# The two ends of a SwiGLU block in an encoder layer: weight sums of the down product formed during gate/up, the first columns of gate/up made earlier, operands of down asked for ahead, the residual added on VectorE

## The chip, the core and the metric

One core of a Trainium2 chip runs the whole layer in one launch. The metric is the device time of that core in microseconds (us). The kernel before takes 3411.99 us in the median of three runs (3408.57 to 3416.47).

## What is computed

One encoder layer over 2304 tokens (a prompt of 2048 and a sample of 256), in float32. With `h = rms_norm(x)`, a combined projection feeds latent attention (8 heads, dense softmax) and a bidirectional SSD scan; their results are mixed by one output projection, and then comes the part that the change is about:

```python
x = x + concat([mla_out, ssd_out]) @ w_out
h = rms_norm(x, ffn_norm_g)
x = x + (silu(h @ w_gate) * (h @ w_up)) @ w_down      # D = 1024, D_FF = 2816
y = rms_norm(x, final_norm_g)
```

## The kernel before

The tokens are 18 tiles of 128. Every float32 product is made from operands that are split in two (a rounded high part, and the rest as a low part), with three matmuls for one (`mm3`, L113 to L115): ScalarE copies the high part, and VectorE subtracts it from the source for the low one (L937 and L938, L1126 and L1127, L1134 and L1135). The stages follow each other; the program is written as one list of operations, each engine gets its own order from a scheduler, and memory that a pool of an earlier stage held is a wait for the later one.

- Projection and scan. Its last tiles store `d_sb` and `d_y` (L564, L569).
- Attention. `load_head` (L654 to L657) loads a head's keys `k` (from `d_k` and `d_kr`) and values; `score` (L113 to L115) makes logits in the two banks `ma` and `mb`, and a reduction takes their maximum `mx` (L679). The pools of this stage lie on the left side of the memory, `mpool` (L613), which holds the attention's output, on the right.
- Output projection, tile by tile: `gather` (L805 to L832) finishes a tile of the scan with two matmuls into bank `o` (L819), `turned` (L840) transposes it through the banks `ta` and `tb`, `project` (L846 to L853) multiplies it by `w_out`, adds the residual and stores the tile in `d_x2`. The first four tiles are also normalised there and stay in memory.
- Gate/up. The tokens are three parts `s` of two halves of three tiles. A Winograd form of Strassen's scheme makes seven products (`MS`), each for the gate and the up weights (`u`), for 11 column blocks `j`: 462 groups of 12 matmuls of 128x384. `turned` (L932, L933) makes the columns `hB0` and `hB1` of a part by 24 transposes for each half through the banks `tb` and `o`, `tokens` (L952 to L963) forms sums of them and splits them into `U`, `weights` (L973 to L992) loads `rawf`, forms sums of it and splits them into `ws`, `group` multiplies (L1005), and `out` (L1026) stores the seven operands of the down product in `d_A`. `weights` runs seven groups ahead.
- Down. Again seven products `m`, in the order 1, 6, 5, 7, 3, 4, 2. Of each, `columns` makes 11 weight blocks `wd`: for 1, 2 and 3 a block as it is loaded (L1105), for 5, 7, 6 and 4 a sum of two, two, three and four blocks, formed on GpSimd (L1114 to L1124). Then nine operands `as` are loaded and split (`operand`, L1132 to L1135), each is multiplied by the 11 blocks (33 matmuls of 128x512), and VectorE adds the result into `acc` (L1147). In `m` = 3 the residual is added, on GpSimd (L1176).

Of the kernel before, what the change touches and what calls it, by code (L numbers as in the profile page):

```python
# [20 lines left out]
P = 128  # L21
D = 1024
# [18 lines left out]
def hymba_kernel(ctx: ExitStack, tc: tile.TileContext, io, seqs, dbg=None):  # L41
# [570 lines left out]
    op = pool(ctx, "e_o", 4, side="right")  # L612
    mpool = pool(mixer, "mla", 1, side="right")  # L613
    mla = {}
# [159 lines left out]


    with ExitStack() as ph:
        st = pool(ph, "d_st", 2)
# [66 lines left out]
        def project(c, mT):  # L844
            xt = mp.tile([P, D], F32, name="xr", tag="xr")
# [16 lines left out]
        first_xs = {}  # L862
        order = [c for c, _ in falling(1)]
        ys, mTs = {}, {}
# [21 lines left out]
    HK = KD // 2  # L886
    G = 3
    W = G * P
    assert NT % (2 * G) == 0
    parts = [(order[i:i + G], order[i + G:i + 2 * G]) for i in range(0, NT, 2 * G)]  # L890
    MS = (1, 2, 6, 5, 3, 7, 4)
    d_A = {(m, s): dram.tile([P, HF, G, P], F32, name=f"d_A{m}_{s}") for m in MS for s in range(len(parts))}


    with ExitStack() as ph:
        hb = pool(ph, "e_hb", 1)
        up = pool(ph, "e_u", 1)
        rp = pool(ph, "e_raw", 3)
        wp = pool(ph, "e_w", 8)
# [22 lines left out]

        H = {}

        def turned(s, half):

            xs = normed(parts[s][half])
            h = hb.tile([P, KD, W], F32, name=f"hB{half}", tag=f"hB{half}")
            for k in range(KD):
                ps = bank(("tb", "o")[k % 2])  # L930
                for i in range(G):
                    nc.tensor.transpose(ps[:, i * P:(i + 1) * P], xs[i][:, k * P:(k + 1) * P], ident)  # L932
                nc.scalar.activation(h[:, k, :], ps[:, :W], AF.Copy, scale=g_ffn[:, k:k + 1])  # L933
            H[s, half] = h

# [134 lines left out]
        for a in groups[:AHEAD]:  # L1070
            weights(*a)
        turned(0, 0)
        tokens(0, 1)
# [17 lines left out]
    with ExitStack() as ph:  # L1091
        rp = pool(ph, "f_raw", 6)
        ap = pool(ph, "f_a", 2)
# [8 lines left out]

        def block(j, i, half):
            raw = rp.tile([P, 512], F32, name="rawd", tag="rawd")
            nc.sync.dma_start(raw, io["w_down"][j + i * HF, :, half * 512:(half + 1) * 512])  # L1105
            return raw

        def columns(m, j):

            if m in (1, 2, 3):  # L1110
                src = block(j, *{1: (0, 0), 2: (1, 0), 3: (1, 1)}[m])
            elif m == 7:
                src, b = block(j, 0, 1), block(j, 1, 1)
                nc.gpsimd.tensor_tensor(src, b, src, op=ALU.subtract)  # L1114
            else:
                b = block(j, 0, 0)
                src = block(j, 0, 1)
                nc.gpsimd.tensor_tensor(src, src, b, op=ALU.subtract)  # L1118
                if m != 5:
                    b = block(j, 1, 1)  # L1120
                    nc.gpsimd.tensor_tensor(src, b, src, op=ALU.subtract)
                if m == 4:
                    b = block(j, 1, 0)
                    nc.gpsimd.tensor_tensor(src, b, src, op=ALU.subtract)  # L1124
            w = wp.tile([P, 2, 512], F32R, name="wd", tag="wd")
            nc.scalar.activation(w[:, 0], src, AF.Copy)  # L1126
            nc.vector.tensor_tensor(w[:, 1], src, f(w)[:, 0], op=ALU.subtract)  # L1127
            return w

        def operand(m, s, t):  # L1130
# [18 lines left out]
        L, R = slice(0, 512), slice(512, 1024)  # L1149
        for m in (1, 6, 5, 7, 3, 4, 2):  # L1150
            cols = [columns(m, j) for j in range(HF)]
            for s, (lo, hi) in enumerate(parts):
                for t in range(G):
                    a = operand(m, s, t)
                    ps = bank("m")
                    for j in range(HF):
                        mm3(ps, a[:, 0, j, :], a[:, 1, j, :], cols[j][:, 0], cols[j][:, 1], j == 0, j == HF - 1)
                    if m == 1:
                        for c in (lo[t], hi[t]):
                            acc[c] = cp.tile([P, D], F32, name=f"acc{c}", tag=f"acc{c}")  # L1160
                    y0, y1 = acc[lo[t]], acc[hi[t]]
                    if m == 1:
                        nc.scalar.activation(y0[:, L], ps, AF.Copy)
                    elif m == 6:
                        add(y1[:, L], ps, y0[:, L])
                    elif m == 5:
                        add(y0[:, R], ps, y1[:, L])
                    elif m == 7:
                        add(y1[:, R], ps, y0[:, R])
                        add(y1[:, L], ps, y1[:, L])  # L1170
                    elif m == 3:
                        add(y0[:, R], ps, y0[:, R])
                        for c in (hi[t], lo[t]):
                            xt = op.tile([P, D], F32, name="o", tag="o")
                            nc.sync.dma_start(xt, d_x2[c])
                            nc.gpsimd.tensor_tensor(acc[c], acc[c], xt, op=ALU.add)  # L1176
                    elif m == 4:
                        add(y1[:, L], ps, y1[:, L])
                        finish(hi[t], y1)
                    else:  # L1180
                        add(y0[:, L], ps, y0[:, L])
                        finish(lo[t], y0)

# [63 lines left out]
```

## Time and profile before

| | |
|---|---|
| median of the runs | 3411.99 us (3408.57, 3411.99, 3416.47) |
| the profiled execution | 3416.36 us, of which the span is 3414.7 us |
| busy over the span | TensorE 95%, VectorE 72%, ScalarE 50%, GpSimd 18% |
| projection and scan | 0 to 745 us |
| attention | 745 to 1619 us |
| output projection | 1619 to 1875 us |
| gate/up | 1875 to 2891 us |
| down | 2891 to 3415 us |

The profiled execution lies 4.4 us above the median, so a time worked out on its trace is 4.4 us too long for the runs. A busy TensorE is shown at the pace of its issue, and the stretches in which it is not busy are the ones to look at: the two at the ends of gate/up, and those in the down product.

### The profile page before, as it was taken

How to read it: one execution, taken by the hardware profiler on the slowest of the kernel's cores; microseconds unless marked ns; L12 is line 12 of the kernel's file. 1: busy time of each engine (PE TensorE's matmuls, PEld its weight loads, DVE VectorE, ACT ScalarE, POOL GpSimd, SP SyncE). 2: the span in 40 equal slices, each digit the busy share in tenths (PEclk: the TensorE clock that was granted, in tenths of full speed). 3: DMA queues.
4: the chain of work that ended last, by engine and by line, in shares of the span. 5: the costliest groups of instructions: out<-in, count | busy, mean ns of one | idle time of the engine just before them, and what ended most of it. 6: DMA issues, size and time to landing. Idle time of an engine off the chain costs nothing.

```text
span 3414.7 us, 48534 instructions
## 1 busy us (share of the span) xinstructions
PE 3244.2 (95%) x17817; PEld 2882.8 (84%) x17817; DVE 2456.1 (72%) x4396; ACT 1698.0 (50%) x3518; POOL 609.4 (18%) x597
## 2 busy tenths in 40 slices
PE   8998999879999999999799799999999999999988
PEld 7897988858888888887688699999999998778777
DVE  6445799978888888887854777787778776354566
ACT  5453444437777777777311545455544444222233
POOL 2222577750000000000310000000000000432630
PEclk9999999979999999999899899999999999999999
DMA  6565222231022111200642333333333333755664
GB/s 253 191 227 186 90 81 75 69 83 37 27 54 52 39 40 41 54 17 15 224 139 99 142 115 122 142 118 118 137 141 132 113 119 118 230 185 172 224 212 137
DMA packets 259166, 407.24 MB, mean 119 GB/s; under 512 B 21424, under 2 KB 170608, under 8 KB 256368
## 3 DMA queue, kind: packets, MB, share of 16 engines
q1 hardware_dynamic: 258928, 404.15, 35.5%
q8 instruction: 140, 2.29, 0.3%
q14 instruction: 98, 0.80, 0.1%
HBM read 274.98 MB, written 129.11 MB: 118 GB/s over the span
## 4 chain that ended last, share of the span: by engine, by line
PE 78%; DVE 11%; DMA 3%; POOL 3%; issue 3%; ACT 2%; SPq 0%; POOLq 0%; ACTq 0%; DVEq 0%
PE bank_mb L1005 8%; PE bank_ma L1005 8%; PE bank_ta L1005 8%; PE bank_ma L113 6%; PE bank_ma L115 6%; PE bank_ma L114 6%; PE bank_mb L113 5%; PE bank_mb L115 5%; PE bank_mb L114 5%; DVE Y L469 4%; PE bank_ta L721 4%; PE bank_o L729 3%; PE bank_o L730 3%; DMA rawd<-w_down 2%; PE bank_tb L721 2%
## 5 line engine op out<-in xcount | busy, mean ns | idle before, releaser
L938 DVE TENSOR_TENSOR ws<-rawf,ws 128x512 fp32r<-128x512 f32 x396 | 267.8, 687 | 97.2 <-ACT ws L937 95.3
L937 ACT ACTIVATE ws<-rawf 128x512 fp32r<-128x512 f32 x396 | 241.8, 627 | 171.7 <-PE bank_ta L1005 37.2
L1005 PE MATMUL bank_ma<-U,ws 128*128 128x384 f32 x1584 | 302.8, 338 | 6.4 <-ACT U L937 3.2
L1005 PE MATMUL bank_mb<-U,ws 128*128 128x384 f32 x1584 | 304.2, 336 | 2.8 <-ACT c L1014 2.5
L1005 PE MATMUL bank_ta<-U,ws 128*128 128x384 f32 x1584 | 297.3, 334 | 3.5 <-ACT U L937 3.0
L1005 PEld LDWEIGHTS bank_ma<-U,ws 128*128 128x128 f32 x1584 | 279.0, 190 | 8.0 <-ACT U L937 3.5
L129 DVE TENSOR_TENSOR pT<-bank_ta,pT 128x512 fp32r<-128x512 f32 (+1 forms) x352 | 239.6, 681 | 63.2 <-ACT pT L128 54.6
L1005 PEld LDWEIGHTS bank_mb<-U,ws 128*128 128x128 f32 x1584 | 277.4, 189 | 5.1 <-ACT c L1014 4.1
L1005 PEld LDWEIGHTS bank_ta<-U,ws 128*128 128x128 f32 x1584 | 276.7, 188 | 4.5 <-ACT U L937 3.3
L128 ACT ACTIVATE pT<-bank_ta 128x512 fp32r<-128x512 f32 (+1 forms) x352 | 209.1, 595 | 116.7 <-PE bank_ta L721 116.2
L1118 POOL TENSOR_TENSOR rawd<-rawd 128x512 f32<-128x512 f32 x33 | 51.5, 1559 | 1189.0 <-DMA rawd<-w_down 1188.6
L729 PE MATMUL bank_o<-pT,v 128*128 128x512 f32 x528 | 248.7, 471 | 1.9 <-ACT ot L736 1.9
L469 DVE SCALAR_TENSOR_TENSOR Y<-X,cw,Y 128x256 f32<-128x256 f32 x288 | 218.5, 815 | 22.9 <-POOL X L456 15.4
L679 DVE TENSOR_REDUCE mx<-bank_ma 128x1 f32<-128x512 f32 (+1 forms) x261 | 177.0, 678 | 50.1 <-PE bank_ma L115 49.5
L721 PE MATMUL bank_ta<-ident,pr 128*128 128x128 f32 x1388 | 210.6, 273 | 2.0 <-DVE pT L129 2.0
L721 PEld LDWEIGHTS bank_ta<-ident,pr 128*128 128x128 f32 x1388 | 170.5, 140 | 48.7 <-DVE pT L129 8.0
L730 PE MATMUL bank_o<-pT,v 128*128 128x512 f32 x528 | 206.2, 391 | 0.0
L1134 ACT ACTIVATE as<-rawa 128x1408 fp32r<-128x1408 f32 x63 | 86.7, 1378 | 225.6 <-PE bank_ma L115 108.6
L688 ACT ACTIVATE pr<-bank_mb,mx 128x512 f32<-128x512 f32 (+1 forms) x261 | 181.4, 695 | 7.9 <-DVE mx L679 4.8
L688 ACT ACTIVATE pr<-bank_ma,mx 128x512 f32<-128x512 f32 (+1 forms) x261 | 179.1, 686 | 6.4 <-DVE mx L707 5.5
L679 DVE TENSOR_REDUCE mx<-bank_mb 128x1 f32<-128x512 f32 (+1 forms) x261 | 176.9, 678 | 7.0 <-PE bank_mb L115 3.7
L752 POOL TENSOR_TENSOR mla<-lo,ri 128x256 f32<-128x256 f32 (+1 forms) x40 | 22.8, 570 | 855.6 <-DVE lo L751 842.5
(399 smaller groups left out, 8584.9 us busy)
## 6 DMA issues: line engine op xcount, KB each, us to landing
rawf<-w_gu SPq DMA_DIRECT2D x66, 1024.0 KB, 5.8
rawa<-d_A SPq DMA_DIRECT2D x63, 704.0 KB, 5.2
rawd<-w_down SPq DMA_DIRECT2D x154, 256.0 KB, 4.9
d_A<-c SPq DMA_DIRECT2D x132, 192.0 KB, 1.9
d_A<-s SPq DMA_DIRECT2D x99, 192.0 KB, 1.9
o<-d_x SPq DMA_DIRECT2D x32, 512.0 KB, 4.8
d_hT<-hT SPq DMA_DIRECT2D x7, 2048.0 KB, 12.9
hT<-d_hT SPq DMA_DIRECT2D x7, 2048.0 KB, 7.9
```

The costliest lines, as they stand in the source:

```text
L113: nc.tensor.matmul(ps, wh, xh, start=start, stop=False)
L114: nc.tensor.matmul(ps, wh, xl, start=False, stop=False)
L115: nc.tensor.matmul(ps, wl, xh, start=False, stop=stop)
L469: nc.vector.scalar_tensor_tensor(y[:, j, :], x[:, j, t:t + n], cw[:, j, t:t + 1], y[:, j, :], op0=ALU.mult, op1=ALU.add)
L679: nc.vector.tensor_reduce(mx[:, j:j + 1], ps[:, :m * P], axis=AX.X, op=ALU.max, negate=nch == 1)
L688: nc.scalar.activation(e[:, :m * P], ps[:, :m * P], AF.Exp, bias=bias, accum_out=rs[:, i, j:j + 1])
L721: nc.tensor.transpose(ps[:, i * P:(i + 1) * P], pr[i, kt // 4][:, kt % 4 * P:(kt % 4 + 1) * P], ident)
L729: nc.tensor.matmul(po[0][:, :n], v[:, s0 + kt, :], pT[:, 0, :n], start=kt == 0, stop=False)
L730: nc.tensor.matmul(po[0][:, :n], v[:, s0 + kt, :], pT[:, 1, :n], start=False, stop=kt == sn - 1)
L937: nc.scalar.activation(dst[:, 0], src, AF.Copy)
L938: nc.vector.tensor_tensor(dst[:, 1], src, f(dst)[:, 0], op=ALU.subtract)
L1005: nc.tensor.matmul(ps[:, :W], w[:, a, k, :], x[:, b, k, :], start=k + n == 0 and not more, stop=k == HK - 1 and n == 2, skip_group_check=more)
```

## The change

It has five parts. (1) The first half's columns are made in the output projection, by `columns_of`, right after the third tile; six tiles are normalised there instead of four, and `mpool` moves to the left side to make room for `hB0`. (2) `sums(j)` loads two rows of blocks of `w_down` during gate/up, forms four sums on GpSimd and stores them in `d_B`; down loads them from there. (3) In down the next operand is asked for one ahead, and the first five weight blocks of the next product two operands ahead of its start. (4) The operands `as` take the room of `hB0` and `hB1`, and the raw blocks get four buffers instead of six. (5) The residual is added on VectorE.

```diff
-    mpool = pool(mixer, "mla", 1, side="right")
+    mpool = pool(mixer, "mla", 1)
...
+    hbs = [pool(ctx, "e_hb0", 1, side="right")]
+    def columns_of(s, half, xs):
+        h = hbs[half].tile([P, KD, W], F32, name=f"hB{half}", tag="hB")
+        for k in range(KD):
+            ps = bank(("tb", "o")[k % 2])
+            for i in range(G):
+                nc.tensor.transpose(ps[:, i * P:(i + 1) * P], xs[i][:, k * P:(k + 1) * P], ident)
+            nc.scalar.activation(h[:, k, :], ps[:, :W], AF.Copy, scale=g_ffn[:, k:k + 1])
+        H[s, half] = h
...
-            if c in order[:4]:
+            if c in order[:2 * G]:
...
+            if c == order[G - 1]:
+                columns_of(0, 0, [first_xs.pop(t) for t in order[:G]])
...
+    hbs.append(pool(ctx, "e_hb1", 1, side="right"))
+    d_B = {m: dram.tile([P, HF, 512], F32, name=f"d_B{m}") for m in (4, 5, 6, 7)}
...
-        hb = pool(ph, "e_hb", 1)
+        rp = pool(ph, "e_raw", 3)
         up = pool(ph, "e_u", 1)
-        rp = pool(ph, "e_raw", 3)
...
+        def sums(j):
+            top, low = (op.tile([P, D], F32, name="o", tag="o") for _ in range(2))
+            nc.sync.dma_start(top, io["w_down"][j])
+            nc.sync.dma_start(low, io["w_down"][j + HF])
+            b11, b12, b21, b22 = top[:, :512], top[:, 512:], low[:, :512], low[:, 512:]
+            for m, out, x, y in ((5, b11, b12, b11), (7, b12, b22, b12), (6, b22, b22, b11), (4, b21, b21, b22)):
+                nc.gpsimd.tensor_tensor(out, x, y, op=ALU.subtract)
+                nc.sync.dma_start(d_B[m][:, j], out)
...
-        turned(0, 0)
...
+            if s + 1 == len(parts) and u and m == 1:
+                sums(j)
...
-        rp = pool(ph, "f_raw", 6)
+        rp = pool(ph, "f_raw", 4)
...
+        def columns(m, j):
             raw = rp.tile([P, 512], F32, name="rawd", tag="rawd")
+            if m in B:
+                i, half = B[m]
+                nc.sync.dma_start(raw, io["w_down"][j + i * HF, :, half * 512:(half + 1) * 512])
             else:
+                nc.sync.dma_start(raw, d_B[m][:, j])
...
-            a = ap.tile([P, 2, HF, P], F32R, name="as", tag="as")
+            a = hbs[n_a[0] % 2].tile([P, 2, HF, P], F32R, name="as", tag="hB")
...
+        prepare(1, AHEAD)
+        ahead = operand(*work[0])
+        for i, (m, s, t) in enumerate(work):
+            prepare(m, HF)
+            a = ahead
+            if i + 1 < len(work):
+                ahead = operand(*work[i + 1])
+            if i % n_m == n_m - 2 and i + 2 < len(work):
+                prepare(work[i + 2][0], AHEAD)
...
-                            nc.gpsimd.tensor_tensor(acc[c], acc[c], xt, op=ALU.add)
+                    nc.vector.tensor_tensor(acc[c], acc[c], xt, op=ALU.add)
```

How the engines' orders move shows at three places. The first is SyncE's queue at the end of the scan, one piece of the difference (`d_sb` and `d_y` are the scan's last stores, `k` and `v` the first head's loads, `q` its queries):

```order
+L564 DMA d_sb_169<-ns_7241 128x512
+L569 DMA d_y_134<-yo 128x512
+L564 DMA d_sb_170<-ns_7291 128x512
 L654 DMA k<-d_k_93 64x4608
 L655 DMA k<-d_kr 32x4608
 L657 DMA v<-d_v 128x18x128
-L569 DMA d_y_130<-yo 128x512
-L564 DMA d_sb_166<-ns_6999 128x512
-L473 DMA d_C_151<-Y 256x1x128
-L473 DMA d_C_152<-Y 256x1x128
```

The loads of the first head now stand behind the last store of the scan, where those of the second head stood; before they stood ahead of its last twelve stores (the rows with a minus are the first four of those).

The second is SyncE's queue in the last but one column blocks of part `s` = 1 of gate/up, of the change (L945 and L946 are the loads of `sums`, L950 its stores, L989 the weights' load, L1042 the stores of `d_A`):

```order
L989 DMA rawf<-w_gu 128x2x1024
L950 DMA d_B_19459<-o 128x512
L946 DMA o<-w_down 128x1024
L950 DMA d_B_19457<-o 128x512
L950 DMA d_B_19458<-o 128x512
L945 DMA o<-w_down 128x1024
L1042 DMA d_A_1_19455<-c_25329 128x384
L946 DMA o<-w_down 128x1024
L950 DMA d_B_19460<-o 128x512
L950 DMA d_B_19459<-o 128x512
```

None of the L945, L946 and L950 rows was there before. Although `sums` is written in part 2, all but the first of the 44 stores stand between the weights of `j` = 7 of part 1 and the end of that part.

The third is SyncE's queue at the start of down (the blocks of `m` = 1 are L1105 before and L1127 in the change, the operands L1132 and L1139, the last stores of gate/up L1026 and L1042). Before:

```order
L1132 DMA rawa<-d_A_0_19353 128x11x128 x2
L1026 DMA d_A_2_19358<-c_28846 128x384
L1105 DMA rawd<-w_down 128x512 x2
L1026 DMA d_A_2_19367<-s_28969 128x384
L1105 DMA rawd<-w_down 128x512 x4
L1132 DMA rawa<-d_A_0_19353 128x11x128
```

And in the change:

```order
L1127 DMA rawd<-w_down 128x512 x4
L1139 DMA rawa<-d_A_0_19436 128x11x128 x3
L1139 DMA rawa<-d_A_1_19437 128x11x128
L1042 DMA d_A_2_19456<-c_29009 128x384
L1042 DMA d_A_2_19447<-s_29096 128x384
L1042 DMA d_A_2_19444<-s_29097 128x384
L1042 DMA d_A_2_19453<-c_29023 128x384
L1127 DMA rawd<-w_down 128x512
L1042 DMA d_A_2_19441<-c_28975 128x384
L1127 DMA rawd<-w_down 128x512 x2
L1042 DMA d_A_2_19450<-s_29098 128x384
L1127 DMA rawd<-w_down 128x512 x2
```

Four operands now stand ahead of the last stores of gate/up, where two stood ahead of the last two of them; the fifth block and the later ones stand among and behind those stores, as the seventh and the later ones did (six had been loaded at the start of part 2).

## Rows read from the trace of the kernel before

**Rows 1.** The page's busy times, shares of the span and instructions of each engine.
```profile
PE 3244.2 (95%) x17817; PEld 2882.8 (84%) x17817; DVE 2456.1 (72%) x4396; ACT 1698.0 (50%) x3518; POOL 609.4 (18%) x597
```
**Rows 2.** The view by stretches of the whole span: stretch, its length, busy time (and count) of TensorE, its weight loads, VectorE, ScalarE and GpSimd, the granted clock, the DMA engines' busy share, GB/s.
```profile
745.00:765.00 20.00, 15.22 (x45) 10.69 (x45) 12.56 (x24) 10.74 (x30) 0.00 (x0) 0.67 0.80 195
765.00:1619.00 854.00, 845.80 (x4801) 692.17 (x4800) 702.98 (x1271) 659.68 (x1633) 21.80 (x38) 1.00 0.14 37
1619.00:1682.00 63.00, 43.97 (x173) 33.24 (x172) 55.05 (x97) 18.68 (x40) 28.81 (x22) 0.81 0.70 236
...
1875.00:1922.00 47.00, 24.49 (x105) 17.97 (x104) 36.23 (x62) 30.38 (x47) 0.00 (x0) 0.75 0.39 148
1922.00:2891.00 969.00, 966.01 (x5585) 962.78 (x5583) 731.46 (x1340) 460.95 (x872) 0.00 (x0) 1.00 0.34 123
2891.00:2906.00 15.00, 7.33 (x18) 5.12 (x17) 11.46 (x16) 8.40 (x12) 0.00 (x0) 0.66 1.06 322
...
2965.00:3000.00 35.00, 28.64 (x112) 22.23 (x111) 18.09 (x17) 11.95 (x16) 13.47 (x10) 0.90 0.75 237
...
3215.00:3295.00 80.00, 65.51 (x259) 50.95 (x258) 45.47 (x54) 20.15 (x25) 62.14 (x32) 0.91 0.80 255
```
**Rows 3.** The timeline of SyncE's queue at the end of the scan (start, length): the first head's keys, and the second head's behind the last store.
```profile
671.53 0.52 SPq L654 DMA_DIRECT2D k<-d_k  x1
...
747.30 0.32 SPq L564 DMA_DIRECT2D d_sb<-ns  x1
747.72 0.51 SPq L654 DMA_DIRECT2D k<-d_k  x1
748.29 0.57 SPq L655 DMA_DIRECT2D k<-d_kr  x1
```
**Rows 4.** The DMA issues from 665 to 700 us (the first head's rotary keys) and from 745 to 765 us (the second's): count, KB, us from issue to landing.
```profile
k<-d_kr SPq DMA_DIRECT2D x1, 576.0 KB, 11.8
...
k<-d_kr SPq DMA_DIRECT2D x1, 576.0 KB, 10.2
```
**Rows 5.** VectorE's timeline where the scan ends: attention's first maximum.
```profile
745.12 0.68 DVE L679 TENSOR_REDUCE mx<-bank_ma 128x1 f32<-128x512 f32 x1
```
**Rows 6.** The chain that ended last, where gate/up starts (start, length, what).
```profile
1874.71 0.24 PE bank_mb L115
...
1876.11 5.29 DMA rawf<-w_gu
...
1918.66 1.68 DVE U L938
1920.38 3.89 PE bank_ma L1005 x11
...
1939.15 4.16 PE bank_ta L1005 x24
```
**Rows 7.** The view by stretches again, of the blocks `j` = 8, 9 and 10 of part 1 and 0 and 1 of part 2 of gate/up.
```profile
2482.30:2511.50 29.20, 29.20 (x168) 29.20 (x169) 20.03 (x35) 12.31 (x24) 0.00 (x0) 1.00 0.46 167
2511.50:2540.60 29.10, 29.10 (x169) 29.10 (x169) 21.27 (x38) 13.49 (x26) 0.00 (x0) 1.00 0.32 119
2540.60:2569.80 29.20, 29.20 (x171) 29.20 (x170) 25.66 (x38) 18.73 (x28) 0.00 (x0) 1.00 0.33 122
2569.80:2599.90 30.10, 29.61 (x169) 28.97 (x168) 28.25 (x39) 14.47 (x26) 0.00 (x0) 1.00 0.44 151
2599.90:2629.10 29.20, 29.20 (x171) 29.20 (x170) 23.98 (x44) 13.73 (x26) 0.00 (x0) 1.00 0.37 137
```
**Rows 8.** Groups of instructions from 3184 to 3277 us, where GpSimd works 89 of 93 us: count, busy time, mean ns of one, idle time before and what ended it.
```profile
L1127 DVE TENSOR_TENSOR wd<-rawd,wd 128x512 fp32r<-128x512 f32 x10 | 19.0, 1912 | 33.0 <-ACT wd L1126 33.0
L1135 DVE TENSOR_TENSOR as<-rawa,as 128x1408 fp32r<-128x1408 f32 x10 | 25.0, 2498 | 1.8 <-ACT as L1134 1.6
L1147 DVE TENSOR_TENSOR acc<-bank_ma,acc 128x512 f32<-128x512 f32 x5 | 3.4, 683 | 5.4 <-PE bank_ma L115 5.4
```
**Rows 9.** The same kind of rows without GpSimd (gate/up's part 2, 2630 to 2860 us, and the operands' splits from 3300 to 3400 us), GpSimd's sums of two blocks over the whole span, and, of 2891 to 3415 us, two groups of 128x1024 (the final scaling, and the residual).
```profile
L938 DVE TENSOR_TENSOR ws<-rawf,ws 128x512 fp32r<-128x512 f32 x96 | 64.7, 688 | 31.5 <-ACT ws L937 31.2
...
L1135 DVE TENSOR_TENSOR as<-rawa,as 128x1408 fp32r<-128x1408 f32 x13 | 21.1, 1626 | 8.7 <-ACT as L1134 8.7
...
L1118 POOL TENSOR_TENSOR rawd<-rawd 128x512 f32<-128x512 f32 x33 | 51.5, 1559 | 1189.0 <-DMA rawd<-w_down 1188.6
...
L1143 DVE SCALAR_TENSOR_TENSOR acc<-acc,rs_y,gf 128x1024 f32<-128x1024 f32 x18 | 23.0, 1285 | 0.5
L1176 POOL TENSOR_TENSOR acc<-acc,o 128x1024 f32<-128x1024 f32 x18 | 52.1, 2904 | 17.5 <-DVE acc L1147 13.4 <-DMA o<-d_x 4.1
```
**Rows 10.** TensorE's timeline where down starts, and two of its last matmuls.
```profile
2886.64 4.67 PE L1005 MATMUL bank_ta<-U,ws 128*128 128x384 f32 x26
2897.88 0.79 PE L113 MATMUL bank_ma<-wd,as 128*128 128x512 f32 x1 [6.57 <-ACT as L1134]
...
3402.80 0.39 PE L114 MATMUL bank_ma<-wd,as 128*128 128x512 f32 x1
...
3405.07 0.39 PE L115 MATMUL bank_ma<-wd,as 128*128 128x512 f32 x1
```
**Rows 11.** The page's DMA issues of the two kinds of load in down: count, KB, us from issue to landing.
```profile
rawa<-d_A SPq DMA_DIRECT2D x63, 704.0 KB, 5.2
rawd<-w_down SPq DMA_DIRECT2D x154, 256.0 KB, 4.9
```

More of the change, by code (lines that the diff above doesn't have):

```diff
@@ L773, in hymba_kernel @@
                 step()
+    G = 3
+    W = G * P
+    assert NT % (2 * G) == 0
+    order = [c for c, _ in falling(1)]
+    parts = [(order[i:i + G], order[i + G:i + 2 * G]) for i in range(0, NT, 2 * G)]
+    hbs = [pool(ctx, "e_hb0", 1, side="right")]
+    H, first_xs = {}, {}
+    def columns_of(s, half, xs):
[6 more added lines that the diff above has]
+        H[s, half] = h
     with ExitStack() as ph:
@@ L844, in project @@
         def project(c, mT):
-            xt = mp.tile([P, D], F32, name="xr", tag="xr")
+            xt = st.tile([P, D], F32, name="xr", tag="rawo")
             nc.sync.dma_start(xt, tile_src[c])
@@ L860, in project @@
                 first_xs[c] = xn
-        first_xs = {}
-        order = [c for c, _ in falling(1)]
+            if c == order[G - 1]:
+                columns_of(0, 0, [first_xs.pop(t) for t in order[:G]])
         ys, mTs = {}, {}
@@ L886, in hymba_kernel @@
     HK = KD // 2
[L887 to L890, printed above, removed]
+    hbs.append(pool(ctx, "e_hb1", 1, side="right"))
     MS = (1, 2, 6, 5, 3, 7, 4)
     d_A = {(m, s): dram.tile([P, HF, G, P], F32, name=f"d_A{m}_{s}") for m in MS for s in range(len(parts))}
+    d_B = {m: dram.tile([P, HF, 512], F32, name=f"d_B{m}") for m in (4, 5, 6, 7)}
     with ExitStack() as ph:
-        hb = pool(ph, "e_hb", 1)
+        rp = pool(ph, "e_raw", 3)
         up = pool(ph, "e_u", 1)
-        rp = pool(ph, "e_raw", 3)
         wp = pool(ph, "e_w", 8)
@@ L921, in normed @@
             return xs
-        H = {}
         def turned(s, half):
[L927 to L934, printed above, removed]
+            columns_of(s, half, normed(parts[s][half]))
+        def sums(j):
[6 more added lines that the diff above has]
+                nc.sync.dma_start(d_B[m][:, j], out)
         def split(dst, src):
@@ L1101, in hymba_kernel @@
         acc = {}
-        def block(j, i, half):
+        B = {1: (0, 0), 2: (1, 0), 3: (1, 1)}
+        def columns(m, j):
             raw = rp.tile([P, 512], F32, name="rawd", tag="rawd")
[L1105 to L1114, printed above, removed]
-            else:
[L1116 to L1124, printed above, removed]
+            if m in B:
+                i, half = B[m]
+                nc.sync.dma_start(raw, io["w_down"][j + i * HF, :, half * 512:(half + 1) * 512])
+            else:
+                nc.sync.dma_start(raw, d_B[m][:, j])
             w = wp.tile([P, 2, 512], F32R, name="wd", tag="wd")
-            nc.scalar.activation(w[:, 0], src, AF.Copy)
-            nc.vector.tensor_tensor(w[:, 1], src, f(w)[:, 0], op=ALU.subtract)
+            nc.scalar.activation(w[:, 0], raw, AF.Copy)
+            nc.vector.tensor_tensor(w[:, 1], raw, f(w)[:, 0], op=ALU.subtract)
             return w
+        n_a = [0]
         def operand(m, s, t):
@@ L1132, in operand @@
             nc.sync.dma_start(raw, d_A[m, s][:, :, t])
-            a = ap.tile([P, 2, HF, P], F32R, name="as", tag="as")
+            n_a[0] += 1
+            a = hbs[n_a[0] % 2].tile([P, 2, HF, P], F32R, name="as", tag="hB")
             nc.scalar.activation(a[:, 0], raw, AF.Copy)
@@ L1149, in hymba_kernel @@
         L, R = slice(0, 512), slice(512, 1024)
[L1150 to L1175, printed above, removed]
-                            nc.gpsimd.tensor_tensor(acc[c], acc[c], xt, op=ALU.add)
[L1177 to L1182, printed above, removed]
@@ new lines, in hymba_kernel, with prepare @@
+        AHEAD = 5
+        work = [(m, s, t) for m in (1, 6, 5, 7, 3, 4, 2) for s in range(len(parts)) for t in range(G)]
+        n_m = len(parts) * G
+        cols = {m: [] for m, _, _ in work}
+        def prepare(m, upto):
+            while len(cols[m]) < upto:
+                cols[m].append(columns(m, len(cols[m])))
+        prepare(1, AHEAD)
+        ahead = operand(*work[0])
+        for i, (m, s, t) in enumerate(work):
+            lo, hi = parts[s]
+            prepare(m, HF)
[4 more added lines that the diff above has]
+                prepare(work[i + 2][0], AHEAD)
+            ps = bank("m")
+            for j in range(HF):
+                mm3(ps, a[:, 0, j, :], a[:, 1, j, :], cols[m][j][:, 0], cols[m][j][:, 1], j == 0, j == HF - 1)
+            if m == 1:
+                for c in (lo[t], hi[t]):
+                    acc[c] = cp.tile([P, D], F32, name=f"acc{c}", tag=f"acc{c}")
+            y0, y1 = acc[lo[t]], acc[hi[t]]
+            if m == 1:
+                nc.scalar.activation(y0[:, L], ps, AF.Copy)
+            elif m == 6:
+                add(y1[:, L], ps, y0[:, L])
+            elif m == 5:
+                add(y0[:, R], ps, y1[:, L])
+            elif m == 7:
+                add(y1[:, R], ps, y0[:, R])
+                add(y1[:, L], ps, y1[:, L])
+            elif m == 3:
+                add(y0[:, R], ps, y0[:, R])
+                for c in (hi[t], lo[t]):
+                    xt = op.tile([P, D], F32, name="o", tag="o")
+                    nc.sync.dma_start(xt, d_x2[c])
+                    nc.vector.tensor_tensor(acc[c], acc[c], xt, op=ALU.add)
+            elif m == 4:
+                add(y1[:, L], ps, y1[:, L])
+                finish(hi[t], y1)
+            else:
+                add(y0[:, L], ps, y0[:, L])
+                finish(lo[t], y0)
```

## The prediction

> **What bounds the kernel now.** I read the page's busy times first: TensorE is busy 95% of the span [rows 1], so the change can win only where TensorE stands still. The view by stretches says where that is [rows 2]. Attention (845.8 of 854 us) and gate/up from 1922 us on (966 of 969) are full. Idle time and a granted clock under 1.00 stand together at four places that the change touches: 745 to 765 us (15.2 of 20 busy, clock 0.67), 1619 to 1682 (44.0 of 63, 0.81), 1875 to 1922 (24.5 of 47, 0.75), and the down product, at its start (7.3 of 15, 0.66) and at two changes of product (28.6 of 35; 65.5 of 80). Then I read the timelines at these places, the chain that ended last, and the stretches of gate/up in which the sums will run, for what VectorE has left there.
>
> **Down: −36.** Two of its last matmuls, 3402.80 and 3405.07 us, lie ten steps apart [rows 10], so 0.227 us each, and 7 x 9 x 11 x 3 = 2079 of them need 472.5 us. The stage takes from 2891.3 (the end of the last group of gate/up, 2886.64 + 4.67) to about 3405.4: 514.1. So 41.6 us are lost: 6.6 before the first matmul (which waits for an operand's split), some 12 at the lower clock after it, about 10 at 2965 to 3000, about 21 at 3215 to 3295, where GpSimd's sums of three and four blocks and the residual run (62.1 of 80 us busy) [rows 2, 10]. The change takes the sums out and has five blocks and an operand ready at each start. A block feeds 3 x 0.227 = 0.68 us, so five last 3.4 us, and twice that where two operands are interleaved; the other six find their room as the last operand of the old product gives it up, one each 0.68 us, and landing takes 4.9 [rows 11]. I leave 2 us at the start, since the fifth block is asked for behind stores of gate/up, and 2 at the other changes. The residual costs VectorE 18 instructions of two memory operands on 128x1024: 1.285 us by the final scaling's row, against 2.904 on GpSimd [rows 9], 23 us in a stretch of about 126 (the products 3 and 4) in which TensorE leads; 2 us for that. −41.6 + 6 = −36; ends −41 (nothing left) and −26 (the start stays half as bad, and the residual delays operands).
>
> **Start of gate/up: −16.** TensorE ends the output projection at 1874.9 and the first `j` at 1943.3 [rows 6]: 68.4 us for 14 groups that take 29.1 later [rows 7]. What ends last: the weights' load, issued at 1876.11 because its room was the projection's, 5.29 us; then VectorE's list up to the last split of `U`, at 1920.3 [rows 6]. After: the load is issued before the last tiles' stores, the first half's columns are made, three tiles less are normalised. VectorE's list from 1875.8 up to the split that the third product needs still holds 22 operations at 0.60 to 0.69, nine on 128x1536 at 1.67 to 1.76, two small ones: about 31 us, so T + 32, where T is the projection's end; behind it ten groups of 2.08 us: T + 52.6 against T + 68.4. Ends: −3 (nothing but the load's 5.3 us less the waits for the second half's columns) and −25.
>
> **Attention's start: +12.5.** Moving one pool gives head 0's keys a room that the scan still uses. Their load was issued at 671.53, and attention's first maximum ran at 745.12, right behind the scan [rows 3, 5]. Now it is queued behind the last store of the scan, where head 1's was, at 747.7 [rows 3]. The rotary half, issued 0.6 us later, took 10.2 and 11.8 us to land [rows 4], so the first product stands at 758.5 to 760, its maximum about 1 us later: +14.4. Some of the stretch before was idle anyway and at the lower clock [rows 2]: 2 less. Attention is full behind it, so nothing is won back. Queued behind this load on SyncE are the values, head 1's keys and queries, which are late by the same. Ends +8 (a landing as short as a block's, 4.9 us) and +17.
>
> **Output projection: +4.** 24 transposes and 8 evictions come from the next stage, the same work. But they take banks `o` and `tb`, of which there is one each, so the scan's matmuls of the seventh tile and the transposes of the fifth wait for them, in a stage whose first 63 us VectorE fills (55 of 63) [rows 2]. Ends −4 and +14.
>
> **The sums: +15.** 44 subtractions of 128x512 on GpSimd, 1.56 us each [rows 9], 22 loads of 512 KB and 44 stores of 256 KB come into gate/up, nearly all in `j` = 8 to 10 of part 1, about 12 to a `j`. GpSimd is idle there, and SyncE holds the weights' loads behind stores that wait for it. What they cost is VectorE's time: while GpSimd works 89 of 93 us, a split of 128x512 takes 1.912 us, and one of the operands 2.498, but an addition with one operand in PSUM 0.683 [rows 8]; without GpSimd the two splits take 0.688 and 1.626 [rows 9]. Two operands in memory therefore wait for GpSimd, and the 20 such operations lost 10 x (1.224 + 0.872) = 21 us by 47 of GpSimd. In gate/up VectorE has 35 to 44 operations per `j`, most of this kind, so here nearly every subtraction will meet one: I take 1 us each, 40 us. VectorE has 9.2, 7.8 and 3.5 us left in `j` = 8 to 10 and 1.9 and 5.2 in the next two [rows 7], and weights are made seven groups (14.6 us) ahead, of which ten are there to be used. 40 − 25 = 15. Bounds: 0 (half a us each, by GpSimd's count in rows 8, fits into the room) and 47 (below).
>
> The Trainium skill ("SBUF — State Buffer", Who interferes with whom) speaks against this part: a VectorE instruction with two inputs in SBUF and a GpSimd one that reads SBUF share a port pair, an exclusive lock, whose loser waits the whole instruction. By that the sum would be the last rival's; rows 8 agree with which operations wait, and no row shows all of the GpSimd time lost.
>
> **Sum:** −36 − 16 + 12.5 + 4 + 15 = −20.5. The profiled execution took 3416.4 us, so 3395.9; it lies 4.4 us above the runs' median of 3412.0, so **3391.5** for the runs.
>
> **The rivals.** From the same sum:
> - *The sums are free*: GpSimd's instructions fall between VectorE's, or VectorE's room suffices. 15 less: 3376.5. For it: GpSimd is used for nothing else there, and the rows show half a us per instruction. Against: `j` = 10 has 3.5 us of room.
> - *The start of gate/up gains only 3*, since VectorE's list is the bound and remains: 13 more, 3404.5. For it: VectorE is busy 36 of 47 us there. Against: its order starts 5.5 us earlier.
> - *The moved columns and the keys cost their upper ends*, +14 and +17: 14.5 more, 3406. For it: one bank of each kind, and a stretch at clock 0.81.
> - *The lock decides, slower*: each of the 44 subtractions holds VectorE up for its whole 1.56 us, 68.6 in all; less 22 of room, 46.6 us of standing TensorE in place of 15: 3423. It decides from a loss of 42 us on (35.5 won elsewhere, and 6.8). For it: rows 8. Against: there VectorE lost half of GpSimd's time at most per operation.
> - *The change doesn't do what it says*: the fifth and later blocks of down come behind stores, and the start stays as it is: +10, inside the ends of down.
>
> The Trainium skill ("Perfetto Trace Analysis", Optimizing Scalar/DVE Operations) says that moving work between GpSimd and VectorE may not help, as they share a port. For the residual the rows decide: it leaves GpSimd, where nothing then runs in down, and this takes the wait out of rows 8 with it.
>
> **How the numbers follow.** A measurement of this kernel tells 0.2% (6.8 us) from no change, so faster is under 3405.2, slower above 3418.8. Chances: the forecast 0.40 (3391.5, itself from 3381 to 3402), free sums 0.18, little at gate/up's start 0.14, upper ends of columns and keys 0.13, the lock 0.15. The range has to reach 3376.5 with down's and the projection's lower ends on that side, 10 us, 3366, and the third and fourth cases with 10 us on the other, 3416; the lock stays outside. Faster: 0.40 less 0.03, 0.18, 0.09 of the second rival, 0.04 of the third: 0.68. Same: 0.03, 0.05, 0.07 and 0.02 of the lock: 0.17. Slower: 0.13 of the lock and 0.02 of the third: 0.15.
>
> **What would show it.** In the changed profile: the first maximum of attention near 759 us instead of 745; the first `j` of gate/up about 52 us after the last matmul of the projection; in `j` = 8 to 10 of part 1 splits of 128x512 well above 0.69 us, VectorE full, and TensorE idle by about 15 us from there into part 2; down at 478 to 482 us from the last group of gate/up to its last matmul, with no idle stretch at 3215's place. The prediction is wrong if gate/up's middle loses over 40 us or nothing, or if down still stands still at its changes of product.

## The result: 0.9% slower

The changed kernel takes 3442.76 us in the median of four runs (3440.36 to 3445.72), the kernel before 3410.28; the ratio is 1.0093 (95% interval 1.0075 to 1.0110). The prediction was 3391.5, 3366 to 3416, with a chance of 0.15 for slower. The profiled execution took 3440.36 us, its span is 3438.6.

Each stage's length is read between ends on TensorE in the two timelines (the last matmul of a stage; for attention's start the first maximum):

| stretch | before | after | forecast | measured |
|---|---|---|---|---|
| first maximum of attention | 745.1 | 762.6 | +12.5 | +17.5 |
| attention's end to projection's end | 255.8 | 266.7 | +4 | +10.9 |
| from there to the end of the first `j` | 68.4 | 52.8 | −16 | −15.6 |
| the other 32 blocks of gate/up | 948.0 | 976.8 | +15 | +28.8 |
| down, from gate/up's last matmul | 514.1 | 496.6 | −36 | −17.5 |

Attention's own length did not change, so its end is 17.5 us late as well; the five together make +24.1, which is the difference of the spans, 23.9, to 0.2 us.

The view by stretches of the changed kernel, with the columns of [rows 2]. Its first row answers to 745 to 765 us there, the next three to 1619 to 1922, the last two to the start of down and what follows; the four from 2496 on answer to [rows 7]:

```profile
746.00:765.00 19.00, 6.10 (x14) 4.40 (x15) 2.07 (x4) 0.60 (x1) 0.00 (x0) 0.50 0.90 209
...
1637.00:1700.00 63.00, 44.40 (x183) 33.03 (x182) 53.18 (x126) 19.66 (x43) 21.86 (x17) 0.86 0.69 235
1700.00:1903.00 203.00, 196.81 (x918) 161.74 (x917) 111.59 (x314) 42.22 (x94) 25.72 (x21) 0.98 0.40 140
1903.00:1956.00 53.00, 39.44 (x194) 36.29 (x193) 46.45 (x60) 30.76 (x46) 0.00 (x0) 0.81 0.25 91
...
2496.00:2525.00 29.00, 29.00 (x168) 29.00 (x169) 19.84 (x24) 10.75 (x22) 18.26 (x12) 1.00 0.87 312
2525.00:2563.00 38.00, 31.67 (x170) 31.35 (x169) 33.72 (x44) 13.74 (x28) 20.89 (x14) 0.91 0.80 294
2563.00:2598.00 35.00, 30.48 (x168) 30.16 (x167) 34.97 (x36) 17.86 (x27) 18.95 (x11) 0.95 0.72 250
2598.00:2640.00 42.00, 32.74 (x170) 31.41 (x169) 37.63 (x45) 16.33 (x28) 19.83 (x7) 0.88 0.64 216
...
2951.00:2962.00 11.00, 6.79 (x21) 4.96 (x22) 5.32 (x5) 4.76 (x6) 0.00 (x0) 0.69 0.72 206
2962.00:3160.00 198.00, 198.00 (x850) 159.56 (x849) 72.00 (x74) 54.89 (x63) 0.00 (x0) 1.00 0.44 131
```

Three readings. At attention's start TensorE now stands (6.1 of 19 us, clock 0.50). The blocks in which GpSimd works (x12, 14, 11 and 7) last 29, 38, 35 and 42 us instead of 29 to 30. And in the last row TensorE is busy for every one of 198 us at full clock, but issues 850 matmuls, 4.29 per us, where [rows 10] have ten in 2.27 us, 4.41 per us: a busy engine that is 3% slower. TensorE's timeline there, two matmuls ten steps apart:

```profile
3099.64 0.40 PE L114 MATMUL bank_ma<-wd,as 128*128 128x512 f32 x1
...
3101.98 0.40 PE L115 MATMUL bank_ma<-wd,as 128*128 128x512 f32 x1
```

2.34 us for ten. Over the whole stage the median step from one matmul to the next is 0.2333 us, against 0.2267 before. That alone is 13.8 us on 2079 matmuls.

### The profile page after: what moved, and what is told of

The parts are those of the page before. It is cut to its first block, busy times and chain, and to the rows that moved or that the text cites. A ratio compares the mean times of both kernels' runs of the same rounds, so it can differ in the third digit from the quotient of the medians.

```text
span 3438.6 us, 48401 instructions
## 1 busy us (share of the span) xinstructions
PE 3263.8 (95%) x17817; PEld 2890.3 (84%) x17817; DVE 2467.8 (72%) x4412; ACT 1697.3 (49%) x3514; POOL 514.2 (15%) x546
## 4 chain that ended last, share of the span: by engine, by line
PE 78%; DVE 13%; DMA 3%; issue 3%; ACT 2%; POOL 1%; SPq 0%; ACTq 0%; DVEq 0%; POOLq 0%
PE bank_ma L1021 7%; PE bank_mb L1021 7%; PE bank_ta L1021 7%; PE bank_ma L113 7%; PE bank_ma L115 7%; PE bank_ma L114 6%; PE bank_mb L113 6%; PE bank_mb L115 5%; PE bank_mb L114 5%; PE bank_ta L721 4%; DVE Y L469 4%; PE bank_o L729 3%; PE bank_o L730 3%; PE bank_tb L721 2%; PE bank_o L1021 2%
## 5 line engine op out<-in xcount | busy, mean ns | idle before, releaser
L954 DVE TENSOR_TENSOR ws<-rawf,ws 128x512 fp32r<-128x512 f32 x396 | 279.6, 717 | 95.2 <-ACT ws L953 93.8
L949 POOL TENSOR_TENSOR o<-o 128x512 f32<-128x512 f32 x44 | 79.2, 1811 | 681.5 <-DMA o<-w_down 666.0
L113 PE MATMUL bank_ma<-hT,wx 128*128 128x256 f32 x576 | 167.1, 290 | 2.2 <-ACT X L445 1.8
```

What stands on the lines that cost most here:

```text
L113: nc.tensor.matmul(ps, wh, xh, start=start, stop=False)
L954: nc.vector.tensor_tensor(dst[:, 1], src, f(dst)[:, 0], op=ALU.subtract)
```

## Experiments

Single runs are compared by their stages' lengths, since single times of the kernel before lay between 3406 and 3416 us.

**Where down's pace comes from.** Two runs move each operand inside its room:

```diff
-            a = hbs[n_a[0] % 2].tile([P, 2, HF, P], F32R, name="as", tag="hB")
+            a = hbs[n_a[0] % 2].tile([P, 2 * HF * P + 16], F32R, name="as", tag="hB")
+            a = a[:, 16:].rearrange("p (a j t) -> p a j t", a=2, j=HF)
```

(16 elements, 64 bytes; in the second run 8 elements.)

> The changed kernel with each operand `as` put 64 bytes further into its room, so that it begins at 32 bytes past a multiple of 128, as in the kernel before, where the changed one has 96. Nothing else differs. Theory A (the address of the operand that is loaded as weights sets the pace of the down matmuls): 0.2333 us per matmul goes back to 0.2267, 13.9 us over 2079 of them, down takes about 483 us instead of 496.6, the whole about 3426 to 3429 us. Theory B (the pace comes from where the rooms of hB0 and hB1 lie, far from the blocks, or from their two rooms' neighbours): the pace stays at 0.2333 and the time within 4 us of the changed kernel's.

> The changed kernel with each operand `as` put 32 bytes further, at a multiple of 128. Theory A: the pace depends on the offset within 128 bytes. If an operand at a multiple of 128 is the cheapest, 0.220 us or less per matmul, which would take 28 us off down (468 us); if only 96 is dear, 0.2267 as with 32. Theory B: 0.2333 as in the changed kernel.

Theory A fell: 0.2325 and 0.2342 us, down 495.5 and 497.7 us. The next two put the operands on the left in the changed kernel (`a = ap.tile(...)`, with the rooms of `hB` closed), and on the right in the kernel before (`pool(ph, "f_as", 2, side="right")`).

> The changed kernel with the operands `as` of down in a pool of their own on the left, between the loads and the weight blocks, as before the change (36512 to 59040 bytes), and the rooms of hB0 and hB1 closed. Offsets within 128 bytes are 32, as in the first run, whose pace stayed at 0.232. Theory C (it is the place of the operands, over 185 KB into a partition and 90 KB or more from the blocks, that sets the pace): 0.2267 us per matmul, 14 us less in down. Theory D (the pace comes from the blocks' place, or from the order of the instructions): 0.232 to 0.234 again, and the time within 4 us of the changed kernel's.

> The kernel before with the operands `as` in a pool on the right side (190432 to 212960 bytes), which also moves the blocks down to 40608; no instruction is changed. Theory C: each matmul of down takes 0.2333 instead of 0.2267 us, down is 14 us longer, 3425 to 3428 us in all. Theory D (order): 0.2267 as before, time within 4 us of before; if the blocks' place is the cause, 0.2333 too.

The pace followed the operands both ways: 0.2267 on the left, 0.2333 in the kernel before with its operands on the right. There down grew from 514.1 to 525.1 us with no instruction changed: 13.8 us by the pace, less 2.8 us of idle time. So the order of the instructions is not the cause. (On the left down took 490.7 us, 6 less than in the changed kernel and not the 14 that I expected. The first matmul waits 6.5 us there for an operand's split, which itself waits 3.3 us for its load.) TensorE ten steps apart, of the first and the second of these two:

```profile
3099.75 0.39 PE L113 MATMUL bank_mb<-wd,as 128*128 128x512 f32 x1
...
3102.02 0.39 PE L114 MATMUL bank_mb<-wd,as 128*128 128x512 f32 x1
```

```profile
3099.80 0.39 PE L113 MATMUL bank_mb<-wd,as 128*128 128x512 f32 x1
...
3102.13 0.39 PE L114 MATMUL bank_ma<-wd,as 128*128 128x512 f32 x1
```

So it is the place, or something that goes with it. Two more runs leave the operands high and shift them by 48 and 112 elements:

> The changed kernel with each operand `as` 192 bytes further into its high room: its start is then, within 512 bytes, where the blocks `wd` start (160). In all stages and kernels so far whose matmuls took the short time (gate/up, the output projection, down before the change and with the operands on the left) the operand that is loaded and the one that is streamed start at the same offset within 512 bytes; in the four slow ones they differ by 320, 384, 352 and 320. Theory F (the difference of the two starts within 512 bytes sets the pace, not the place): 0.2267 us per matmul though the operands lie at 188 to 212 KB, 14 us less than the changed kernel, 3426 to 3430 us. Theory C (the high place): 0.232 to 0.234.

> The same with 448 bytes, so that the two starts differ by 256 within 512 bytes. Theory F with a period of 256 bytes: 0.2267 as well. With a period of 512: 0.230 or more. Theory C: 0.232 to 0.234.

Theory C fell, and theory F held, with a period of 256 bytes: 0.2267 us in both. Down took 485.6 and 485.7 us, 11 less than in the changed kernel: 13.8 by the pace, of which 2.8 stand idle elsewhere in the stage. The first of these runs took 3432.1 us in all, above the 3426 to 3430 expected, because its attention began later (first maximum at 767.4 us). Its timeline:

```profile
3099.61 0.39 PE L114 MATMUL bank_ma<-wd,as 128*128 128x512 f32 x1
...
3101.88 0.39 PE L115 MATMUL bank_ma<-wd,as 128*128 128x512 f32 x1
```

| kernel | operand's start, mod 256 | block's start, mod 256 | apart | us per matmul |
|---|---|---|---|---|
| before; operands on the left | 160 | 160 | 0 | 0.2267 |
| shifted by 192 and by 448 bytes | 160 | 160 | 0 | 0.2267 |
| changed; before with operands high | 224 | 160 | 64 | 0.2333 |
| shifted by 64 bytes | 32 | 160 | 128 | 0.2325 |
| shifted by 32 bytes | 0 | 160 | 96 | 0.2342 |

In all these kernels the blocks start at 160. The runs alone therefore leave a rival: that the operand's own start sets the pace, with 160 a good one and 224 a bad one. The trace of the kernel before speaks against it. In the projection of its first stage the weights `wz` and the columns `hT` both start at 224 within 256 bytes, and ten steps take 2.27 us there too:

```profile
222.32 0.39 PE L114 MATMUL bank_mb<-wz,hT 128*128 128x512 f32 x1
...
224.59 0.39 PE L115 MATMUL bank_mb<-wz,hT 128*128 128x512 f32 x1
```

**The sums.** The first run leaves out the 44 subtractions (the line with `gpsimd.tensor_tensor`); the second puts them on VectorE; the third holds each pair of loads to one block of part 2:

```diff
+            nc.scalar.activation(top[:, :1], C["c11", 1][:, :1], AF.Copy)
             nc.sync.dma_start(top, io["w_down"][j])
```

> The changed kernel without the 44 subtractions of `sums` (the blocks are stored in d_B as they were loaded, so down uses wrong sums); all loads and stores of `sums` stay. Theory P (VectorE loses the time to GpSimd's reads): the four slow blocks j = 9, 10 of part 1 and 0, 1 of part 2 of gate/up go from 38.0, 35.3, 42.0 and 30.0 us to 29.1, 29.1, 30.2 and 29.1, 28 us less in all, and VectorE's splits of 128x512 take 0.69 us there. Theory Q (the weights' loads come late, since SyncE's queue holds them behind stores and loads of `sums`): with the stores no longer waiting for GpSimd part of that goes, but the transfers stay: 10 to 20 of the 28 us remain, with waits for rawf.

> The changed kernel with the 44 subtractions of `sums` on VectorE. They still stand in j = 7 to 10 of part 1. Theory P (the loss comes from VectorE and GpSimd at the same operands' port): 44 x 0.69 = 30 us of VectorE's own time in place of 80 us of GpSimd's; the room in these blocks is some 20 us, so 5 to 12 us of the 28 remain. Theory Q (SyncE's queue and the transfers): the stores now wait for VectorE's list instead of GpSimd, as many of them, 20 us or more remain.

> The changed kernel with `sums` held to one j of part 2 each: ScalarE copies one column of the block's first result into the room of the first load, which the load then has to wait for. GpSimd still does 44 subtractions, now four in each of the eleven blocks, in which VectorE has 6.2 us left of 29.1. Theory P with a loss of about 1 us each: 4 to 5 us a block, inside what is left, so gate/up loses under 5 us in all and the whole takes 3414 to 3420 us. Rival (each subtraction costs TensorE its own time wherever it stands, since weights are late whenever VectorE is): 28 us or more are lost as before, spread over part 2.

The 32 blocks took 958.3, 962.3 and 955.2 us: 10.3, 14.3 and 7.2 over the kernel before, where the changed kernel has 28.8. What stays in the first run is the lower end of theory Q's range; what stays in the second lies between the two theories. Without the subtractions 18.5 us go, so they, with the stores that wait for them, are most of it; but 10 stay that need no GpSimd at all. The view by stretches of this run, blocks `j` = 7 to 9 of part 1, shows the loads and stores then pressed into three blocks (DMA share 0.64, 0.94 and 0.80). Block `j` = 7 takes 39.3 us, where the kernel before (first row; its next two stand in [rows 7]) has 32.5, and the chain waits 8.38 us there for one load of weights (last row):

```profile
2449.80:2482.30 32.50, 32.00 (x194) 31.51 (x192) 28.75 (x78) 19.95 (x44) 0.00 (x0) 1.00 0.32 114
```

```profile
2466.00:2505.30 39.30, 34.70 (x195) 33.14 (x193) 29.98 (x82) 19.98 (x45) 0.00 (x0) 0.96 0.64 227
2505.30:2534.50 29.20, 29.20 (x168) 29.20 (x169) 14.68 (x25) 8.87 (x17) 0.00 (x0) 1.00 0.94 345
2534.50:2565.10 30.60, 29.48 (x170) 29.09 (x169) 27.28 (x48) 15.81 (x31) 0.00 (x0) 1.00 0.80 305
```

```profile
2486.00 8.38 DMA rawf<-w_gu
```

With the sums on VectorE two blocks stay slow, the second of them 41.5 us. Held to one block each, GpSimd's work costs next to nothing in nine blocks of eleven (29.1 to 29.7 us each). In the first block, where VectorE is fullest, 1.9 us are lost, and in the last, into which down's first loads fall, 4.5:

```profile
2588.10:2620.10 32.00, 30.22 (x169) 28.95 (x168) 30.42 (x37) 14.64 (x27) 9.09 (x4) 1.00 0.43 151
2620.10:2883.10 263.00, 262.69 (x1515) 262.06 (x1514) 204.39 (x334) 115.87 (x227) 53.92 (x36) 1.00 0.56 188
2883.10:2916.80 33.70, 31.08 (x170) 30.70 (x169) 16.50 (x25) 12.73 (x23) 5.98 (x4) 0.95 0.81 264
```

Its time, 3427.5 us, missed the 3414 to 3420 that I gave: gate/up lost 7.2 us where I had under 5, down took 3.3 us longer than in the changed kernel (499.9), and attention and projection were over 5.6 us later, as they vary between single runs. The rival fell too: 7.2 us are lost and not 28. So it is the burst that costs, 43 of the 44 sums with their loads and stores in four blocks.

**Attention's start.** The kernel before with `mpool` on the left and nothing else.

> The kernel before with one line of the change: the pool `mla` on the left side. Theory: head 0's keys then wait for the scan's last stores, so attention's first maximum comes at 760 to 763 us instead of 745, every later stage is 15 to 18 us late, and the whole takes 3426 to 3430 us; output projection, gate/up and down keep their lengths to 2 us. Rival (the late start comes from another part of the change, and the pool alone costs nothing): within 4 us of the kernel before.

3436.2 us beside 3413.0. SyncE's timeline and VectorE's first maximum:

```profile
752.01 0.32 SPq L564 DMA_DIRECT2D d_sb<-ns  x1
752.43 0.61 SPq L654 DMA_DIRECT2D k<-d_k  x1
...
766.15 0.69 DVE L679 TENSOR_REDUCE mx<-bank_ma 128x1 f32<-128x512 f32 x1 [16.45 <-PE bank_ma L115]
```

One line delays attention by 21 us, and nothing behind it makes it up: projection, gate/up and down keep their lengths (254.5, 1015.2 and 513.7 us). That is more than the 15 to 18 us expected. But the start varies between single runs: in the other nine profiles with this pool on the left and no repair of it the first maximum stands between 756.6 and 767.4 us, and in the changed kernel above at 762.6. So 17.5 and 21 us are not two different losses.

**The early columns.** In the changed kernel:

```diff
-            ps = bank(("tb", "o")[k % 2])
+            ps = bank("tb" if s + half == 0 else ("tb", "o")[k % 2])
```

> The changed kernel with the early columns made through bank `tb` alone, so that bank `o` stays free for the matmuls of `gather`. The output projection of the changed kernel takes 266.7 us from the end of attention, 10.9 more than before, of which 3 are the 24 transposes. Theory G (the scan's matmuls queue behind the columns in bank `o`, and everything of later tiles behind them): 5 to 8 us of that go, 259 to 262 us. Rival (bank `tb`, or VectorE's and ScalarE's work, holds it up): 265 us or more.

260.4 us, 6.3 less, where nine profiles with both banks have 266.5 to 269.2: bank `o` was what held the stage up. The view by stretches, against the second and third row of the changed kernel's above:

```profile
1638.00:1701.00 63.00, 46.95 (x183) 35.09 (x182) 54.90 (x103) 19.77 (x42) 29.39 (x22) 0.78 0.74 242
1701.00:1898.00 197.00, 193.93 (x921) 160.75 (x920) 103.80 (x337) 42.10 (x96) 19.25 (x16) 1.00 0.41 142
```

**All four repaired.** The room of head 0 is opened first, and the other three edits come from above (the sums in `j` = 1 to 9 of part 2):

```diff
-        lp = pool(ph, "c_l", 2)
-        qp = pool(ph, "c_q", 2)
         kvs = [pool(ph, "c_kv0", 1)]
+        qp = pool(ph, "c_q", 2)
+        lp = pool(ph, "c_l", 2)
```

> The changed kernel with four repairs, each from a run before: head 0's room for keys and values is opened first in attention, so that it lies over projection weights again (67168 to 94816 bytes) and its load goes out during the scan; the early columns use bank `tb` alone; the operands `as` start 192 bytes further (the start of the blocks within 256 bytes); the sums are held to the blocks j = 1 to 9 of part 2. If the losses are the separate ones that the runs showed, they add up: first maximum of attention at 745 to 748 us (17 less than the changed kernel), output projection 260 us (6 less), gate/up's middle within 3 us of the kernel before (26 less), 0.2267 us per matmul in down (11 to 14 less). Together 60 to 63 us less than the changed kernel's 3442.8: 3378 to 3385 us, 0.8 to 1.0% under the kernel before. Rival (they share a cause, or one bottleneck only gives way to the next): 3395 us or more.

3376.81 us (3376.34 to 3377.84), 66 less than the changed kernel and 0.9892 of the kernel before (0.9875 to 0.9908). The parts add up, and the whole is 1.2 us under the range given: first maximum at 745.9, projection 259.2, first `j` 52.4, the other blocks 949.8, down 485.9 us. So the four losses are separate ones.

**The start of down.** What was left there, in the kernel with four repairs:

```diff
+                if m == 6 and j < AHEAD:
+                    nc.scalar.activation(raw[:, :1], acc[parts[1][0][0]][:, :1], AF.Copy)
                 nc.sync.dma_start(raw, d_B[m][:, j])
```

> The kernel of the run before (four repairs) with the first five blocks of down's second product held back: the load of each waits for one column that ScalarE copies from the fourth operand's result. In the changed kernel and in the run before ScalarE splits 16 blocks in a row at the start of down, five of them for the second product, and the third operand's split stands behind them (its matmuls waited 4.6 us for it, at a granted clock of 0.72 afterwards). If that is what the start still loses, the first product of down takes 4 to 8 us less and the whole 3369 to 3373 us. Rival (the blocks of the first product themselves come too late, or the operand's load): within 2 us of the run before, 3375 to 3379 us.

3371.30 us (3368.44 to 3372.92), 0.9874 of before (0.9857 to 0.9890). Down's first product took 73.9 us instead of 77.8. At full pace it would take 67.3, so 3.9 of 10.5 us are explained by this, and 6.6 stay open. TensorE's waits for the operands' splits at 2880 to 2912 us (count, busy, mean ns, idle and what ended it), without and with the edit:

```profile
L113 PE MATMUL bank_ma<-wd,as 128*128 128x512 f32 x21 | 9.4, 447 | 4.7 <-ACT as L1145 4.7
```

```profile
L113 PE MATMUL bank_ma<-wd,as 128*128 128x512 f32 x21 | 9.0, 429 | 1.5 <-ACT as L1147 1.5
```

## Why the prediction was wrong

The forecast had the right sign at all five places. It was right in size at one, too small at the three losses, and twice too large at the main gain; the errors all point the same way, 44 us in all.

**Down (−36, measured −17.5): the step "2079 of them need 472.5 us" failed.** It carried the pace of [rows 10] over to a kernel whose operands lie elsewhere. At 0.2333 they need 485.1, and neither my terms nor the end of −26 held a price for a moved buffer. (The sum had two slips of little weight. At 0.227 the product is 471.9. And the places listed for the 41.6 us make 49.6, because the "some 12 at the lower clock" is 4.3 in the trace: the first product took 71.6 us, at full pace 67.3.) The second miss is "2 us at the start": it was 9.1 (the first product took 78.4 us, a full-pace one 69.3). I looked at SyncE's queue, where the fifth block stands behind stores, and not at ScalarE's, where the blocks of the next product, asked for early, stand ahead of the third operand. The last experiment shows about 4 us of the miss to be this; the rest of it is not explained. In the changed kernel:

```profile
2952.34 0.63 ACT L1131 ACTIVATE wd<-rawd 128x512 fp32r<-128x512 f32 x1 [0.38 <-DMA rawd<-d_B]
2952.87 0.58 ACT L1185 ACTIVATE acc<-bank_ma 128x512 f32<-128x512 f32 x1
2953.35 1.37 ACT L1142 ACTIVATE as<-rawa 128x1408 fp32r<-128x1408 f32 x1
```

What asks ahead takes a place in the line of every engine that it passes. The rest was right: the other changes of product and the residual lost 2.4 us against 4, the residual's additions take 1.225 us on VectorE against the 1.285 that I took, and the blocks' splits went from a mean of 0.953 us to 0.687 with GpSimd silent:

```profile
L1132 DVE TENSOR_TENSOR wd<-rawd,wd 128x512 fp32r<-128x512 f32 x77 | 50.1, 687 | 33.8 <-ACT wd L1131 33.8
...
L1198 DVE TENSOR_TENSOR acc<-acc,o 128x1024 f32<-128x1024 f32 x18 | 22.0, 1225 | 15.7 <-DMA o<-d_x 15.3
```

**The sums (+15, measured +28.8): "40 − 25" failed, above all in its second number.** In the four blocks VectorE was busy 126.2 us against 95.2 in [rows 7], 31 more for 44 sums, 0.7 us each where I took 1. Of the 25 us of room it used only some 5: it stood idle for 22.4 us of these blocks before and still for 17.8 now. The room is there while VectorE waits for weights, and they came late as well (the last row below). The groups from 2525 to 2640 us, answering to [rows 8, 9]:

```profile
L954 DVE TENSOR_TENSOR ws<-rawf,ws 128x512 fp32r<-128x512 f32 x38 | 33.2, 886 | 2.8 <-ACT ws L953 2.7
L954 DVE TENSOR_TENSOR U<-hB,U 128x1536 fp32r<-128x1536 f32 x7 | 14.8, 2107 | 0.0
...
L1035 DVE TENSOR_TENSOR c<-bank_ta,c 128x384 f32<-128x384 f32 x11 | 6.0, 550 | 0.0
...
L999 DVE TENSOR_TENSOR S<-rawf 128x512 f32<-128x512 f32 x6 | 5.2, 868 | 5.8 <-DMA rawf<-w_gu 5.8
```

and the chain at the stall of `j` = 9, where the weights' load goes out behind a load and a store of the sums and then takes 6.84 us ([rows 6] have 5.29):

```profile
2547.14 1.48 SPq L945
2548.67 0.42 SPq L950
...
2549.18 6.84 DMA rawf<-w_gu
```

I had named SyncE's queue in a clause and given it no price. In number this came between the forecast and the rival of the lock, but that rival as I priced it is not it: VectorE lost 0.7 us to a subtraction, and not the 1.56 that one lasts in [rows 9]. The Trainium skill ("SBUF — State Buffer", Who interferes with whom) holds for which operations wait: those with one operand in PSUM took 0.550 us, while the splits, with both in memory, went from 0.688 [rows 9] to 0.886. How long the loser of its lock waits these sums do not show: GpSimd's own 44 subtractions took 1.29 to 6.91 us here, 1.81 in the mean, so some of the waiting may be GpSimd's.

**Attention's start (+12.5, measured +17.5): the mechanism was right, its size too small.** The load went out at 749.4, behind a last store that itself came 1.7 us later than before. The first product followed 11 us after the issue of the rotary half, between the two landings of [rows 4], of which my +14.4 took the lower, and the maximum 1.7 us behind it instead of 1. The 2 us that I took off for idle time before were not given back: from the first maximum on attention took 874.1 us, against 874.0. SyncE's, TensorE's and VectorE's timelines:

```profile
748.99 0.32 SPq L564 DMA_DIRECT2D d_sb<-ns  x1
749.42 0.52 SPq L654 DMA_DIRECT2D k<-d_k  x1
749.99 0.58 SPq L655 DMA_DIRECT2D k<-d_kr  x1
...
760.94 0.76 PE L113 MATMUL bank_ma<-k,q 96*128 96x512 f32 x1 [12.66 <-issue]
...
762.60 0.69 DVE L679 TENSOR_REDUCE mx<-bank_ma 128x1 f32<-128x512 f32 x1 [15.91 <-PE bank_ma L115]
```

**Projection (+4, measured +10.9): the mechanism was right, its size too small.** Bank `o` makes 6.3 us of it; I had put it near the middle of bounds that reach to +14. The other 4.6 us were not taken apart. They hold the moved work, and perhaps a line that the difference above does not show: the tile of the residual, `xr`, now takes the room of the raw weights, `rawo`.

**The start of gate/up (−16, measured −15.6) was right in its mechanism**, counted along VectorE's list in its new order; that it also agrees to 0.4 us is luck. The split that the third product waits for ended 29.9 us after the projection, where I had 32, and the groups behind it took 22.9 us, where I had 20.8, because the first of them ran at a lower pace (3.89 us for eleven matmuls), as it does in [rows 6]:

```profile
1931.64 1.68 DVE U L954
1933.36 3.89 PE bank_ma L1021 x11
```

**The chances.** The unfavourable cases were drawn as alternatives, each beside a forecast for all else. They are independent losses at different places, as the four repairs show, and three came at once; the range, made of one case at a time, could not hold that.

## What to carry to other kernels

A buffer's address is part of a change: list which buffers move, what earlier owner each now waits for (one pool's side cost 17 to 21 us here), and whether a matmul's two operands still start at the same offset within 256 bytes (13.8 us of down here). Work that is put into another stage's idle time should be held to the block that has the room, because a scheduler lets it go as early as its buffers allow, in one burst. Count what is asked for ahead on every queue it enters, and add up losses at separate places instead of choosing among them.

## What was not expected of the hardware

A matmul of 128x512 in down took 0.2267 us where the operand that is loaded and the operand that is streamed start at the same offset modulo 256 bytes in their partitions, and 0.2325 to 0.2342 us where they start 64, 96 or 128 bytes apart; the busy time and the granted clock (1.00) show nothing of it. It was measured for these two operands in this layout (all their pieces at multiples of 512 bytes from the start); why the offsets matter is not settled. Other products of the kernel before, matched with their addresses in the order of the program, show less of it: `hT` by `wa` (432 columns) takes 0.194 us in the median at 0 apart and 0.196 at 64, 128 and 192, and attention's `q` by `k` (96 rows, 512 columns) 0.232 at 0 and 0.233 at 192. So equal offsets are no promise of the short time everywhere, and what a shift is worth has to be measured for each shape.
